# Gate one-hots by pairs of tokens, more U tiles called in the gate steps, dot products of gathered rows behind the V splits

## The chip, the cores and the metric

The kernel is one program on one core of a Trainium2 chip. A core has five engines that run their own instruction streams: TensorE (PE; its weight loads are listed as PEld), VectorE (DVE), ScalarE (ACT), GpSimd (POOL) and SyncE (SP), which issues most DMAs. The metric is the device time of one execution in microseconds (us); less is better. Before the change, three runs gave a median of 2682.41 us (2677.13 to 2683.87).

## The reference

The reference is two transformer blocks on 512 tokens of 1024 features, in fp32. The change touches the last part of the first block, a layer of 16384 experts with one row each in two tables U and V:

```
q = (x @ w_query) -> 8 heads x 2 halves;   s = q . sub_keys        # 128 scores each
top 16 of each half, their 16 x 16 sums, top 16 of those           # 8 heads x 16 experts per token
g = softmax(best);  a = gelu(u[experts] . x);  out = sum(g * a * v[experts])
```

So each token takes 128 of the 16384 experts with weights g. The second block (attention, a recurrence, cross attention and a mixture of 32 experts) isn't touched.

## The kernel before, in words

The expert layer is computed in two ways. For the first three blocks of 128 tokens (384 tokens, `TD`) it is dense: a matrix G of gate weights, 16384 experts by 384 tokens, mostly zero, is built; then U times x, Gelu, times G, and that times V, for all experts. For the fourth block it is sparse: for each of the 128 expert slots of a token, the U row is gathered by an indirect DMA (one row per token, 128 x 1024 numbers) and its dot product with the token is taken on VectorE; later the V row is gathered and added with its weight. That makes 256 gathered rows, in four buffers, the four blocks of the tile `x_sb`.

**Gate steps** (L1172 to L1211). A token's G column is 128 x 128 (the expert's number in two halves), a sum over its 128 slots of products of two one-hot vectors. It is a matmul: the slots lie on the partitions, `oj` is the one-hot of the one half and `o1`, `o2` that of the other times the two parts of the weight. A one-hot of 128 is in turn the product of a one-hot of 8 and one of 16 (the "digits", `digit`, for three chunks of 32 tokens at a time). One step does 8 tokens: three VectorE products (L1197), 16 matmuls of 128 x 128 fp16 (L1205, L1206), two evictions of four tokens each on ScalarE into the staging tile `g_sg` (L1208). 48 steps make 12 chunks; each chunk's 2 MB of `g_sg` go to DRAM (L1211), with two staging tiles. Layout before: four tokens side by side in memory, then the next of the 128 places, so a matmul that takes one token reads fp16 numbers 8 bytes apart. After each third step `u_tile()` is called.

**U tiles** (`u_tile`, L881). One U tile is 128 experts: 512 KB are loaded (three buffers), split into a high part on ScalarE and a low part `w_lo` on VectorE (two buffers each), multiplied in 24 matmuls of 384 columns into PSUM (`b_ups`, two buffers), and Gelu'd on ScalarE into one of 46 places: 10 in `x_sb`, which the gathers need later, and 36 in `b_ab`. A place is free again when the V tile of that number has multiplied it with its gates (`b_wfull`, L945). There are 128 U tiles; 28 calls stand in the program ahead of the gate steps (12 in the selection of the best, 4 and 12 after it), 16 in the gate steps, and a loop fills up to 46.

**V tiles** (`for n in range(128)`, L990 on). Round n loads 512 KB of V (and for each fourth round 768 KB of G), multiplies (`b_wfull`), splits both factors (the low part of V is `b_vl`, on VectorE), and runs 18 matmuls of 512 columns. From round 10 on it also calls `u_tile()`, which does nothing once 128 are done, and then lets gathered rows through: 2.72 a round until round 91, then 1.2, each a gather on POOL's queue (L914) and a dot product (L921) or an addition (L931) on VectorE.

**What sets the order.** The framework schedules at compile time. Each engine's order is worked out from a cost model: of the instructions whose inputs and buffers are there, the one written first in the program goes first, and one that waits for a buffer lets later ones pass. The order is then fixed, and an engine waits in it. Two tools pin an instruction: `keep_in_program_order(i)` puts i behind the instruction of the same engine that was written just before it, and `issue_after(j)` puts all of a block's instructions on j's engine behind j. Both set the order of issue alone. The rows' dot products have the first kind:

```
r = row("u_rows", k)
tc.keep_in_program_order(V.scalar_tensor_tensor(
    junk[:], r, 1.0, h2g[:], op0=OP.mult, op1=OP.mult, accum_out=ag[:, k:k + 1]))
```

Of the kernel before, what the change touches and what calls it, by code (L numbers as in the profile page):

```python
# [13 lines left out]
FP16 = mybir.dt.float16  # L14
# [3 lines left out]
OP = mybir.AluOpType  # L18
# [35 lines left out]
class Kern:  # L54
# [14 lines left out]

    def split(self, src, hi, lo):  # L70
        self.nc.scalar.copy(hi, src)  # L71
        self.nc.vector.tensor_tensor(lo, src, hi, op=OP.subtract)  # L72

    def mm3(self, ps, a, b, start, stop):
        mm = functools.partial(self.nc.tensor.matmul, skip_group_check=True)
# [753 lines left out]
GT = 32  # L829
OG = 8  # L830
DG = 3
# [27 lines left out]
def phase_b(K):  # L859
    nc, tc, d = K.nc, K.tc, K.d  # L860
    V, S, PE = nc.vector, nc.scalar, nc.tensor
    with ExitStack() as st:
        pb = st.enter_context(tc.tile_pool(name="b_pb", bufs=1))
        hT = K.hT
        h2g = K.h2g
        eg = pb.tile([128, 128], I32, name="b_eg")
        gg3 = pb.tile([128, 128], F32, name="b_gg3")
        ag = pb.tile([128, 128], F32, name="b_ag")
# [30 lines left out]
        with ExitStack() as s2:  # L899
# [7 lines left out]
            junk = jp.tile([128, 1024], BF16, name="b_junkg")  # L907
            acc = [[vps.tile([128, 512], F32, name=f"b_acc{b}{h}") for h in range(2)] for b in range(ND)]
            nrow = [0]

            def row(src, k):
                r = K.x[:, nrow[0] % NB]
                nrow[0] += 1
                nc.gpsimd.indirect_dma_start(out=r, out_offset=None, in_=d[src],  # L914
                                             in_offset=bass.IndirectOffsetOnAxis(ap=eg[:, k:k + 1], axis=0))
                return r

            def gather_steps():
                for k in range(128):
                    r = row("u_rows", k)  # L920
                    tc.keep_in_program_order(V.scalar_tensor_tensor(  # L921
                        junk[:], r, 1.0, h2g[:], op0=OP.mult, op1=OP.mult, accum_out=ag[:, k:k + 1]))
                    yield
                S.activation(ag[:], ag[:], AF.Gelu)
                V.tensor_tensor(ag[:], ag[:], gg3[:], op=OP.mult)
                for k in range(128):
                    r = row("v", k)
                    if k == 0:
                        V.tensor_scalar(accg[:], r, ag[:, 0:1], None, op0=OP.mult)
                    else:  # L930
                        tc.keep_in_program_order(V.scalar_tensor_tensor(  # L931
                            accg[:], r, ag[:, k:k + 1], accg[:], op0=OP.mult, op1=OP.add))
                    yield
# [3 lines left out]
            def weighted(n, halves):  # L937

                if n % 4 == 0:
                    g4s[n // 4] = gp.tile([128, TD // GT, 4, GT], F32, name="b_g")  # L940
                    nc.sync.dma_start(g4s[n // 4][:].rearrange("p c i t -> p c (i t)"), gd[n // 4])
                raw = vr.tile([128, 1024], F32, name="b_vraw")
                nc.sync.dma_start(raw[:], d["v"][n * 128:(n + 1) * 128, :])
                f = wf.tile([128, TD], F32, name="b_wfull")
                V.tensor_tensor(f[:].rearrange("p (c t) -> p c t", t=GT), acts[n].rearrange("p (c t) -> p c t", t=GT),  # L945
                                g4s[n // 4][:, :, n % 4], op=OP.mult)
                wh = wsp.tile([128, TD], F32R, name="b_wh")
                wl = wsp.tile([128, TD], F32R, name="b_wl")
                K.split(f[:], wh[:], wl[:])
                vh, vl = halves  # L950
                K.split(raw[:], vh[:], vl[:])
                return wh, wl, vh, vl

            def add_rows(n, t, b, hf):
# [4 lines left out]
            def v_halves():  # L959
                return vs.tile([128, 1024], F32R, name="b_vh"), vs.tile([128, 1024], F32R, name="b_vl")  # L960
# [28 lines left out]
            gs = gather_steps()  # L989
# [4 lines left out]
            for n in range(128):  # L994
                if n < 128 - NLAST:
                    t = weighted(n, v_halves())
# [21 lines left out]
            with in_order(tc):  # L1018
# [4 lines left out]
                f = [finish(b, (accg, h2g)[b % 2], gf, gm, vr.tile([128, 1024], F32, name="b_vraw")) for b in range(ND)]  # L1023
# [4 lines left out]
def peer_gates(K, st, P, hT, small, gd, eg, gg3, u_tile):  # L1028
    nc, tc, d = K.nc, K.tc, K.d
    V, S, PE = nc.vector, nc.scalar, nc.tensor  # L1030
    tk = st.enter_context(tc.tile_pool(name="g_tk", bufs=1))
    tT = tk.tile([128, 6, TD], FP16, name="g_tT")
    rt = tk.tile([128, 16, 16], FP16, name="g_rt")
    with ExitStack() as s0:
# [4 lines left out]
        with ExitStack() as s1:  # L1039
# [18 lines left out]
            for hp in range(16):  # L1058
                w, ps = began.pop(0)
# [25 lines left out]
        for b in range(NB):  # L1085
# [3 lines left out]
            for i in range(5):  # L1089
                n = LENS[i]  # L1090
# [15 lines left out]
        n = NB * 128  # L1106
# [32 lines left out]
        for b in range(NB):  # L1139
# [15 lines left out]
            if b < ND:  # L1155
# [5 lines left out]
                hi = tt[:].bitcast(F32).rearrange("p (a n) -> p a n", a=2)  # L1161
# [5 lines left out]
    with ExitStack() as s2:  # L1167
        ohp = s2.enter_context(tc.tile_pool(name="g_ohp", bufs=2))
        stg = s2.enter_context(tc.tile_pool(name="g_stg", bufs=2))
        gps = s2.enter_context(tc.tile_pool(name="g_gps", bufs=4, space=PSUM))  # L1170
        dg = s2.enter_context(tc.tile_pool(name="g_dg", bufs=1))
        G4 = DG * GT // 4  # L1172
        for c in range(TD // GT):
            if c % DG == 0:
                ts = slice(c * GT, (c + DG) * GT)
                token = lambda w: tT[:, w, ts].rearrange("p (g t) -> p g t", t=4)[:, :, None, :]

                def digit(w, n):

                    t = dg.tile([128, G4, n, 4], FP16, name=f"g_d{w}")  # L1180
                    V.tensor_tensor(t[:], token(w).to_broadcast(t[:].shape),
                                    rt[:, None, 0:n, 0:4].to_broadcast(t[:].shape), op=OP.is_equal)
                    return t[:]

                ih, jh, il, jl = digit(0, 8), digit(1, 8), digit(2, 16), digit(3, 16)
                ih0, ih1 = [dg.tile([128, G4, 8, 4], FP16, name=f"g_d{w}")[:] for w in (4, 5)]
                for w, t in ((4, ih0), (5, ih1)):
                    V.tensor_tensor(t, ih, token(w).to_broadcast(t.shape), op=OP.mult)
            sg = stg.tile([128, 128, GT], F32, name="g_sg")
            for t8 in range(GT // OG):  # L1190
                g0 = ((c % DG) * GT + t8 * OG) // 4
                gs = slice(g0, g0 + OG // 4)
                shape = [128, OG // 4, 8, 16, 4]

                def onehot(hi, lo, name):
                    t = ohp.tile([128, OG // 4, 128, 4], FP16, name=name)
                    V.tensor_tensor(t[:].rearrange("p g (a b) t -> p g a b t", a=8), hi[:, gs, :, None].to_broadcast(shape),  # L1197
                                    lo[:, gs, None].to_broadcast(shape), op=OP.mult)
                    return t

                oj, o1, o2 = onehot(jh, jl, "g_oj"), onehot(ih0, il, "g_o1"), onehot(ih1, il, "g_o2")
                for g in range(OG // 4):
                    ps = gps.tile([128, 4, 128], F32, name="g_gp")
                    for t in range(4):
                        PE.matmul(ps[:, t], oj[:, g, :, t], o1[:, g, :, t], start=True, stop=False)  # L1205
                        PE.matmul(ps[:, t], oj[:, g, :, t], o2[:, g, :, t], start=False, stop=True)  # L1206
                    tq = t8 * OG + 4 * g
                    S.activation(sg[:, :, tq:tq + 4].rearrange("p i t -> p t i"), ps[:], AF.Copy, scale=1.0 / GS)  # L1208
                if (c * (GT // OG) + t8) % 3 == 0:
                    u_tile()  # L1210
            nc.sync.dma_start(gd[:, :, c].rearrange("q p n -> p q n"), sg[:].rearrange("p (q i) t -> p q (i t)", i=4))  # L1211

# [1078 lines left out]
def build(tc, d, out, phases="abcd"):  # L2291
# [3 lines left out]
    with ExitStack() as st:  # L2295
# [16 lines left out]
        with ExitStack() as s1:  # L2312
            if "a" in phases or "b" in phases:
                p2 = s1.enter_context(tc.tile_pool(name="p2", bufs=1))
                K.colsa = p2.tile([128, 27], F32, name="colsa")
                nc.sync.dma_start(K.colsa[:], d["colsa"])
                K.gt2 = p2.tile([128, 1024], F32, name="gt2")
                K.A2 = p2.tile([128, 8], F32, name="A2")
                K.sh2 = p2.tile([128, 8], F32, name="sh2")
                K.h2g = p2.tile([128, 1024], F32, name="h2g")  # L2320
                K.ur = s1.enter_context(tc.tile_pool(name="ur", bufs=3))
                K.us = s1.enter_context(tc.tile_pool(name="us", bufs=2))
                K.xd = s1.enter_context(tc.tile_pool(name="xd", bufs=1, space=DRAM)).tile([NB, 128, 1024], F32, name="xd")
            if "a" in phases:
                phase_a(K)
            elif "b" in phases:
                nc.sync.dma_start(K.gt2[:], bcast_rows(d["gt2_t"], 1024))
                nc.sync.dma_start(K.A2[:], d["A2_t"])
                nc.sync.dma_start(K.sh2[:], d["sh2_t"])
            if "b" in phases:  # L2330
                phase_b(K)
# [28 lines left out]
```

## Time and profile before

| what | value |
|---|---|
| median of three runs | 2682.41 us |
| the profiled execution | 2687.5 us |
| its span, first to last instruction | 2685.7 us |
| mean granted TensorE clock | 0.973 |
| busy: PE, DVE, ACT, POOL | 2548.9, 1782.5, 962.9, 395.8 us |
| gate steps (first to last matmul) | 598.2 to 756.2 us |
| V tiles (first to last matmul) | 774.1 to 1646.3 us |

Times in the rows are us from the span's start unless marked ns. A matmul's record holds its time in the pipe, so neighbours overlap; what one costs in a stream is the distance from start to start. VectorE's records overlap by some 80 ns in the same way. "<-" behind an idle time names what ended it.

### The profile page before, as it was taken

Reading aid. Unit: us, or ns where it says so; the run is one execution under the profiler, and the core shown is the slowest. Engines: PE = TensorE matmul, PEld = TensorE weight load, DVE = VectorE, ACT = ScalarE, POOL = GpSimd, SP = SyncE. Lnnn points to the kernel's source line nnn. Section 1 sums busy time; section 2 is a strip of 40 time slices with the busy share of each in tenths; the row PEclk is TensorE's granted clock in tenths of the full one; section 3 lists DMA queues with packets and bytes.
Section 4 is the critical chain, followed back from the end, with each engine's and each line's share of the span. In section 5 each row is a group of like instructions: output and inputs, shape, how many; then the busy total and the mean of one; then the engine's idle time right before and its main releaser. Section 6 shows DMA issues by size and latency. Waiting matters only on the chain.

```text
span 2685.7 us, 43758 instructions
## 1 busy us (share of the span) xinstructions
PE 2548.9 (95%) x17112; PEld 2122.0 (79%) x17112; DVE 1782.5 (66%) x3794; ACT 962.9 (36%) x1603; POOL 395.8 (15%) x269
## 2 busy tenths in 40 slices
PE   5999999899999999999999998999999989999885
PEld 4976988899978999999999887888797756555664
DVE  6644689987756788778878797567753673333334
ACT  3431442457743333333333335343533421111112
POOL 0000000000013555545555320000000000000001
PEclk8999999999999999999999998898999999999998
DMA  6226222336787989989998883222133489999896
GB/s 232 79 92 210 103 73 80 104 126 188 219 285 273 328 318 329 327 320 323 323 330 317 296 312 122 81 85 74 56 119 114 176 326 387 394 396 360 340 416 260
DMA packets 183485, 623.93 MB, mean 232 GB/s; under 512 B 15847, under 2 KB 66407, under 8 KB 156651
## 3 DMA queue, kind: packets, MB, share of 16 engines
q1 hardware_dynamic: 146410, 486.87, 48.5%
q0 software_dynamic: 36864, 134.23, 14.4%
q8 instruction: 135, 2.21, 0.3%
q14 instruction: 76, 0.61, 0.1%
HBM read 591.55 MB, written 29.49 MB: 231 GB/s over the span
## 4 chain that ended last, share of the span: by engine, by line
PE 83%; DVE 10%; DMA 3%; ACT 2%; issue 2%; SPq 0%; DVEq 0%; ACTq 0%
PE f_hp L1865 6%; PE b_acc L77 6%; PE b_acc L78 6%; PE b_acc L76 6%; PE b_ups L78 6%; PE b_ups L76 6%; PE b_ups L77 6%; PE p_acc L77 5%; PE p_acc L76 5%; PE p_acc L78 5%; PE f_yp L1907 3%; PE f_xp L1764 2%; PE g_gp L1205 2%; PE g_gp L1206 2%; PE f_hp L1851 1%
## 5 line engine op out<-in xcount | busy, mean ns | idle before, releaser
L72 DVE TENSOR_TENSOR w_lo<-w_raw,w_hi 128x1024 fp32r<-128x1024 f32 x228 | 278.0, 1219 | 248.3 <-ACT w_hi L71 248.0
L71 ACT CAST w_hi<-w_raw 128x1024 fp32r<-128x1024 f32 x228 | 239.0, 1048 | 548.4 <-PE b_ups L77 280.9
L78 PE MATMUL b_ups<-hT,w_lo 128*128 128x384 f32 x1024 | 347.8, 340 | 6.6 <-DVE w_lo L72 6.5
L76 PE MATMUL b_ups<-hT,w_hi 128*128 128x384 f32 x1024 | 347.8, 340 | 1.3 <-ACT x_sb L891 1.0
L77 PE MATMUL b_ups<-hT,w_hi 128*128 128x384 f32 x1024 | 345.1, 337 | 0.0
L914 POOL DMA_INDIRECT x_sb<-in_u_rows,b_eg x128 | 197.0, 1539 | 994.5 <-ACT w_hi L71 774.7
L77 PE MATMUL b_acc<-b_vl,b_wh 128*128 128x512 f32 x756 | 297.0, 393 | 9.4 <-DVE b_vl L72 9.3
L76 PE MATMUL b_acc<-b_vh,b_wh 128*128 128x512 f32 x756 | 295.1, 391 | 1.3 <-ACT b_vh L71 1.3
L78 PE MATMUL b_acc<-b_vh,b_wl 128*128 128x512 f32 x756 | 296.1, 392 | 0.0
L77 PE MATMUL p_acc<-w_lo,hT 128*128 128x256 f32 x896 | 255.0, 285 | 7.7 <-DVE w_lo L72 7.7
L76 PE MATMUL p_acc<-w_hi,hT 128*128 128x256 f32 x896 | 255.4, 285 | 2.0 <-ACT hT L71 1.8
L78 PE MATMUL p_acc<-w_hi,hT 128*128 128x256 f32 x896 | 254.3, 284 | 0.0
L914 POOL DMA_INDIRECT x_sb<-in_v,b_eg x128 | 188.6, 1473 | 217.9 <-DVE b_accg L931 189.5
L78 PEld LDWEIGHTS b_ups<-hT,w_lo 128*128 128x128 f32 x1024 | 193.8, 189 | 8.6 <-DVE w_lo L72 8.6
L76 PEld LDWEIGHTS b_ups<-hT,w_hi 128*128 128x128 f32 x1024 | 194.0, 189 | 5.1 <-ACT x_sb L891 1.3
L77 PEld LDWEIGHTS b_ups<-hT,w_hi 128*128 128x128 f32 x1024 | 193.6, 189 | 3.2
L77 PEld LDWEIGHTS p_acc<-w_lo,hT 128*128 128x128 f32 x896 | 171.8, 192 | 13.7 <-DVE w_lo L72 8.2
L71 ACT CAST b_wh<-b_wfull 128x384 fp32r<-128x384 f32 x128 | 65.6, 514 | 320.1 <-PE b_acc L77 314.9
L76 PEld LDWEIGHTS p_acc<-w_hi,hT 128*128 128x128 f32 x896 | 171.5, 192 | 7.6 <-issue 3.9
L78 PEld LDWEIGHTS p_acc<-w_hi,hT 128*128 128x128 f32 x896 | 171.7, 192 | 4.2 <-issue 3.4
L921 DVE SCALAR_TENSOR_TENSOR b_junkg<-x_sb,h2g 128x1024 bf16<-128x1024 f32 x128 | 156.3, 1221 | 25.7 <-DMA x_sb<-in_u_rows,b_eg 24.1
L77 PEld LDWEIGHTS b_acc<-b_vl,b_wh 128*128 128x128 f32 x756 | 142.9, 189 | 38.1 <-DVE b_vl L72 11.1
(659 smaller groups left out, 5101.6 us busy)
## 6 DMA issues: line engine op xcount, KB each, us to landing
f_w<-in_w SPq DMA_DIRECT2D x192, 1024.0 KB, 10.4
w_raw<-in_u SPq DMA_DIRECT2D x128, 512.0 KB, 5.6
b_vraw<-in_v SPq DMA_DIRECT2D x128, 512.0 KB, 6.5
b_gd<-g_sg SPq DMA_DIRECT2D x12, 2048.0 KB, 9.1
b_g<-b_gd SPq DMA_DIRECT2D x32, 768.0 KB, 8.0
a_ar_t<-in_w_ada SPq DMA_DIRECT2D x32, 512.0 KB, 4.3
w_raw<-in_w_tok SPq DMA_DIRECT2D x20, 512.0 KB, 3.6
a_ar_t<-in_w_ada SPq DMA_DIRECT2D x8, 1024.0 KB, 8.2
```

Source lines behind the costliest of these rows:

```text
L71: self.nc.scalar.copy(hi, src)
L72: self.nc.vector.tensor_tensor(lo, src, hi, op=OP.subtract)
L76: first = mm(ps, a[0], b[0], start=start, stop=False)
L77: mm(ps, a[0], b[1], start=False, stop=False)
L78: mm(ps, a[1], b[0], start=False, stop=stop)
L914: nc.gpsimd.indirect_dma_start(out=r, out_offset=None, in_=d[src], in_offset=bass.IndirectOffsetOnAxis(ap=eg[:, k:k + 1], axis=0))
L921: tc.keep_in_program_order(V.scalar_tensor_tensor(junk[:], r, 1.0, h2g[:], op0=OP.mult, op1=OP.mult, accum_out=ag[:, k:k + 1]))
L1205: PE.matmul(ps[:, t], oj[:, g, :, t], o1[:, g, :, t], start=True, stop=False)
L1206: PE.matmul(ps[:, t], oj[:, g, :, t], o2[:, g, :, t], start=False, stop=True)
L1764: PE.matmul(room[k // 4][:, k % 4, :n], hs[i][:, b, k * 128:(k + 1) * 128], sel[:, b, :n], start=k % 4 == 0 and i == 0 and b == 0, stop=i ...
L1865: last = PE.matmul(p, X[:, k], ts["w31", k // 2][:, c0:c0 + 512], start=k == 0, stop=k == 7, skip_group_check=True)
L1907: PE.matmul(p, gT[k], ts["w2", hf][:, k * 512:(k + 1) * 512], start=k == 0, stop=k == 3, skip_group_check=True)
```

## The change

Three edits. The gate one-hots and their digits are laid out with two tokens side by side instead of four, so that a matmul reads numbers 4 bytes apart; the number of elements per VectorE instruction and the matmuls stay. `u_tile()` is called after four of five gate steps (38 calls) instead of one of three (16). And `split` returns its VectorE instruction, the V split's is kept in `split[0]`, and the rows' U dot products are also put behind it with `issue_after`.

```
     def split(self, src, hi, lo):
         self.nc.scalar.copy(hi, src)
-        self.nc.vector.tensor_tensor(lo, src, hi, op=OP.subtract)
+        return self.nc.vector.tensor_tensor(lo, src, hi, op=OP.subtract)
...
+            split = [None]
...
                     r = row("u_rows", k)
-                    tc.keep_in_program_order(V.scalar_tensor_tensor(
-                        junk[:], r, 1.0, h2g[:], op0=OP.mult, op1=OP.mult, accum_out=ag[:, k:k + 1]))
+                    with tc.issue_after(split[0].ins):
+                        tc.keep_in_program_order(V.scalar_tensor_tensor(
+                            junk[:], r, 1.0, h2g[:], op0=OP.mult, op1=OP.mult, accum_out=ag[:, k:k + 1]))
...
-                K.split(raw[:], vh[:], vl[:])
+                split[0] = K.split(raw[:], vh[:], vl[:])
...
-                token = lambda w: tT[:, w, ts].rearrange("p (g t) -> p g t", t=4)[:, :, None, :]
+                token = lambda w: tT[:, w, ts].rearrange("p (g t) -> p g t", t=2)[:, :, None, :]
...
-                    t = dg.tile([128, G4, n, 4], FP16, name=f"g_d{w}")
+                    t = dg.tile([128, GN, n, 2], FP16, name=f"g_d{w}")
...
-                shape = [128, OG // 4, 8, 16, 4]
+                shape = [128, OG // 2, 8, 16, 2]
...
-                    t = ohp.tile([128, OG // 4, 128, 4], FP16, name=name)
+                    t = ohp.tile([128, OG // 2, 128, 2], FP16, name=name)
...
-                    for t in range(4):
-                        PE.matmul(ps[:, t], oj[:, g, :, t], o1[:, g, :, t], start=True, stop=False)
-                        PE.matmul(ps[:, t], oj[:, g, :, t], o2[:, g, :, t], start=False, stop=True)
+                    for q in range(4):
+                        j, t = divmod(4 * g + q, 2)
+                        PE.matmul(ps[:, q], oj[:, j, :, t], o1[:, j, :, t], start=True, stop=False)
+                        PE.matmul(ps[:, q], oj[:, j, :, t], o2[:, j, :, t], start=False, stop=True)
...
-                if (c * (GT // OG) + t8) % 3 == 0:
+                if (c * (GT // OG) + t8) % 5:
                     u_tile()
```

## Rows read from the trace of the kernel before

**Rows 1.** By stretch: length, busy (count) of PE, PEld, DVE, ACT, POOL, clock, DMA share, GB/s.
```profile
598.20:756.40 158.20, 158.20 (x1156) 149.78 (x1156) 115.31 (x172) 118.09 (x130) 0.00 (x0) 1.00 0.67 203
...
774.10:843.20 69.10, 59.70 (x241) 47.92 (x242) 44.31 (x66) 22.36 (x32) 18.05 (x14) 0.93 0.79 295
...
790.70:796.30 5.60, 5.59 (x13) 4.48 (x14) 2.58 (x4) 0.00 (x0) 1.88 (x2) 0.50 0.81 300
...
847.30:1498.70 651.40, 651.40 (x3317) 595.17 (x3316) 520.65 (x649) 228.26 (x317) 335.14 (x215) 1.00 0.90 323
```

**Rows 2.** The chain of waits between the stages: start, us, what.
```profile
757.55 9.29 DMA b_gd<-g_sg
767.00 4.55 DMA b_g<-b_gd
...
780.73 7.46 DMA x_sb<-in_u_rows,b_eg
```

**Rows 3.** VectorE in order of time, at three places of the V stage.
```profile
803.95 0.56 DVE L945 TENSOR_TENSOR b_wfull<-b_a,b_g 128x384 f32<-128x384 f32 x1
...
847.43 1.23 DVE L72 TENSOR_TENSOR w_lo<-w_raw,w_hi 128x1024 fp32r<-128x1024 f32 x1 [2.46 <-ACT w_hi L71]
848.57 1.22 DVE L921 SCALAR_TENSOR_TENSOR b_junkg<-x_sb,h2g 128x1024 bf16<-128x1024 f32 x1
...
1508.09 1.22 DVE L72 TENSOR_TENSOR b_vl<-b_vraw,b_vh 128x1024 fp32r<-128x1024 f32 x1
1509.23 1.28 DVE L931 SCALAR_TENSOR_TENSOR b_accg<-x_sb,b_ag,b_accg 128x1024 f32<-128x1024 f32 x1
```

**Rows 4.** ScalarE in order of time: start, us, engine, line, what, idle time before.
```profile
761.18 0.49 ACT L891 ACTIVATE b_a<-b_ups 128x384 f32<-128x384 f32 x1
...
765.34 0.49 ACT L891 ACTIVATE b_a<-b_ups 128x384 f32<-128x384 f32 x1
...
804.54 0.49 ACT L891 ACTIVATE b_a<-b_ups 128x384 f32<-128x384 f32 x1 [1.65 <-DVE b_wfull L945]
```

**Rows 5.** TensorE in order of time: two gate matmuls, and L1764.
```profile
752.25 0.28 PE L1205 MATMUL g_gp<-g_o,g_oj 128*128 128x128 f16 x1
...
755.91 0.29 PE L1206 MATMUL g_gp<-g_o,g_oj 128*128 128x128 f16 x1
...
2195.64 3.75 PE L1764 MATMUL f_xp<-f_sel,f_hs 128*128 128x128 f16 x64
```

**Rows 6.** Weight loads of the gate matmuls and of L1764: ns min/median/max.
```profile
L1205 PEld LDWEIGHTS <-g_oj x384: 113/117/138, 598.2 to 755.7; 128*128 128x128 f16 x192
...
L1764 PEld LDWEIGHTS <-f_hs x896: 95/98/181, 2162.5 to 2609.7; 128*128 128x128 f16 x180
```

**Rows 7.** Groups by shape in the gate stage, VectorE and ScalarE; then four evictions together.
```profile
L1197 DVE TENSOR_TENSOR g_o<-g_d,g_d 128x1024 f16<-128x1024 f16 x96 | 61.8, 683 | 0.0
...
L1181 DVE TENSOR_TENSOR g_d<-g_tT,g_rt 128x1536 f16<-128x1536 f16 x8 | 7.4, 957 | 0.0
L1181 DVE TENSOR_TENSOR g_d<-g_tT,g_rt 128x768 f16<-128x768 f16 x8 | 4.4, 563 | 0.0
L1188 DVE TENSOR_TENSOR g_d<-g_d,g_tT 128x768 f16<-128x768 f16 x8 | 4.1, 549 | 0.0
...
753.61 3.92 ACT L1208 ACTIVATE g_sg<-g_gp 128x512 f32<-128x512 f32 x4
```

**Rows 8.** Windows of L921 (two records per row), then of L931 (one).
```profile
774.10:843.20 69.10, 12.30 (x20) 0.93 0.79 295
843.20:1437.00 593.80, 145.02 (x236) 1.00 0.90 322
...
843.20:1437.00 593.80, 97.23 (x76) 1.00 0.90 322
```

**Rows 9.** DMA issues by line: engine, count, us from issue to landing.
```profile
x_sb<-in_v,b_eg POOLq DMA_INDIRECT x128, 7.3
```

**Rows 10.** The page, part 5: line, what, count, busy us, mean ns, idle before.
```profile
L914 POOL DMA_INDIRECT x_sb<-in_v,b_eg x128 | 188.6, 1473 | 217.9 <-DVE b_accg L931 189.5
```

More of the change, by code (lines that the diff above doesn't have):

```diff
@@ L1171, in peer_gates @@
         dg = s2.enter_context(tc.tile_pool(name="g_dg", bufs=1))
-        G4 = DG * GT // 4
+        GN = DG * GT // 2
         for c in range(TD // GT):
@@ L1175, in peer_gates @@
                 ts = slice(c * GT, (c + DG) * GT)
-                token = lambda w: tT[:, w, ts].rearrange("p (g t) -> p g t", t=4)[:, :, None, :]
+                token = lambda w: tT[:, w, ts].rearrange("p (g t) -> p g t", t=2)[:, :, None, :]
                 def digit(w, n):
-                    t = dg.tile([128, G4, n, 4], FP16, name=f"g_d{w}")
+                    t = dg.tile([128, GN, n, 2], FP16, name=f"g_d{w}")
                     V.tensor_tensor(t[:], token(w).to_broadcast(t[:].shape),
-                                    rt[:, None, 0:n, 0:4].to_broadcast(t[:].shape), op=OP.is_equal)
+                                    rt[:, None, 0:n, 0:2].to_broadcast(t[:].shape), op=OP.is_equal)
                     return t[:]
                 ih, jh, il, jl = digit(0, 8), digit(1, 8), digit(2, 16), digit(3, 16)
-                ih0, ih1 = [dg.tile([128, G4, 8, 4], FP16, name=f"g_d{w}")[:] for w in (4, 5)]
+                ih0, ih1 = [dg.tile([128, GN, 8, 2], FP16, name=f"g_d{w}")[:] for w in (4, 5)]
                 for w, t in ((4, ih0), (5, ih1)):
@@ L1190, in peer_gates @@
             for t8 in range(GT // OG):
-                g0 = ((c % DG) * GT + t8 * OG) // 4
-                gs = slice(g0, g0 + OG // 4)
-                shape = [128, OG // 4, 8, 16, 4]
+                g0 = ((c % DG) * GT + t8 * OG) // 2
+                gs = slice(g0, g0 + OG // 2)
+                shape = [128, OG // 2, 8, 16, 2]
                 def onehot(hi, lo, name):
-                    t = ohp.tile([128, OG // 4, 128, 4], FP16, name=name)
+                    t = ohp.tile([128, OG // 2, 128, 2], FP16, name=name)
                     V.tensor_tensor(t[:].rearrange("p g (a b) t -> p g a b t", a=8), hi[:, gs, :, None].to_broadcast(shape),
```

## The prediction

> **What bounds the kernel now.** I read the page's first part first: TensorE is busy for most of the span, so nearly everything that is saved has to be TensorE time or TensorE idle time. Then the table by stage [rows 1], which holds the two stages that the change touches. In the gate stage (598.2 to 756.4) TensorE is busy 158.2 of 158.2 us at full clock, VectorE 115.3 and ScalarE 118.1: TensorE bounds it. At the head of the V stage (774.1 to 843.2) TensorE is busy only 59.7 of 69.1 us and the mean granted clock is 0.93; after that, in 847.3 to 1498.7, busy all the time, with the DMA engines at 0.90 and 323 GB/s.
>
> In the chain of waits the gate stage ends in a DMA to DRAM and one back (9.29 and 4.55 us), and the head of the V stage in a gathered row that lands 7.46 us after its issue [rows 2]. The order on VectorE [rows 3] shows what ties a row's dot product: it comes right behind `w_lo` of the U tile that is called in the same round (847.43, 848.57), and, when no U tile is left, right behind `b_vl` of the round (1508.09, 1509.23). That is `keep_in_program_order`: an edge to the VectorE instruction written just before. It decides this forecast.
>
> Unit prices. A U tile is 4.16 us of TensorE (two neighbours, 761.18 and 765.34) [rows 4]. A pair of U and V tile is 8.25 us (651.4 us for 79 pairs) [rows 1], so a V tile is 4.09. A gate matmul is 0.118 us: 31 steps from 752.25 to 755.91 [rows 5].
>
> **Part 1, pairs of tokens.** 768 gate matmuls now step 8 bytes from column to column, then 4. The nearest fp16 matmuls of the same size, L1764, read neighbouring columns: 64 in 3.75 us, 0.058 each [rows 5]. The weight load hardly differs between the two (117 and 98 ns) [rows 6], so I put the doubling down to the moving operand. [...] A gate step of 16 falls from 1.89 to 0.93 us.
> [...]
> VectorE writes the same number of elements per one-hot, 683 ns [rows 7]. No row has an inner run of two. [...]
>
> **Part 2, U tiles in the gate steps.** 28 U tiles stand in the program ahead of the gate steps. `% 5` calls 38 in 48 steps, `% 3` called 16. But only 46 outputs have a place (10 in `x_sb`, 36 in `b_ab`), and two more wait in PSUM: already now the Gelu of the 47th waits for the product of V tile 10 (804.54 behind 803.95) [rows 3, 4]. So 48 U tiles are multiplied ahead of the V stage before and after. In the program numbers 28 to 47 now fall into the first 25 steps: 20 x 4.16 + 25 x 0.93 = 106.4 us, from 598.2 to 704.6. The 23 steps left have no U tile. VectorE: 23 x 3 x 0.60 (683 ns less the 80 by which its records overlap) + 4.0 for one group of digits ((7.4 + 4.4 + 4.1)/4) = 45.4 us; ScalarE: 46 evictions of 0.98 (3.92 for four) = 45.1 [rows 7]; the writes of `g_sg`, two buffers, some 8 us to fill and 9.29 to land, (8 + 9.3)/2 = 8.65 per four steps, 49.7. I take 49.7: the last eviction ends at 754.3 instead of 757.55. Bounds 45 (750) and, with a matmul of 0.118, 131 + 50 from 598.2 (779). Halving the gate matmuls thus gives 3.3 us, as the steps without U tiles are not TensorE's. The DMA pair of 16.6 us until the first V matmul (774.14) is covered now by four U tiles and then by nothing; it costs no more, but TensorE starts cold: 2.6 us, as between 790.7 and 796.3, where the clock was 0.50 and 13 matmuls took 0.43 instead of 0.23 [rows 1].
>
> **Part 3, dot products behind the V split.** Before, 10 rows came into the first 13 V tiles [rows 8], because the U tile of their round (46 to 49) had long been split. Those rows made the stalls: 69.1 us for 13 x 4.09 = 53.2, so 15.9 lost, and all of it goes. But not by the new edge. In round 10 the program now calls U tile 66, not 46, so the first dot product stands behind `w_lo` of U tile 66. That needs tile 64 multiplied, thus 62's Gelu, thus the product of V tile 26, which runs when TensorE is in V tile 21 (tile 10's ran at 803.95 in V tile 5: 93 matmuls of 18 each had started). U tiles run 8 rounds earlier than now (48 after V tile 4, now after 12), and the rows some 11 rounds later. The edge to `b_vl` is weaker and binds nowhere.
>
> So 16 pairs pass with no gather on the DMA queues. Rows of round n stand behind U tile 56 + n up to round 71; when the last `w_lo` (U 127) is done, TensorE is in V tile 82, and 62 x 2.72 = 168 rows have been let through. TensorE gets there at 754.3 + 16.6 + 2.6 + 83 x 4.09 + 79 x 4.16 = 1441.6. Before, at 1437, 10 + 118 + 76 = 204 rows were done [rows 8].
>
> The rest is 45 V tiles, one U tile and 88 rows. TensorE alone: 45 x 4.09 + 4.16 = 188, done at 1630, 16 before the 1646 of now. VectorE: 88 x 1.2 + 45 x (1.14 + 2 x 0.47) = 199 [rows 3]. DMA: 88 x 0.524 MB + 42 x 0.721 MB (three V tiles are loaded by then; 0.524 of V, a fourth of 0.786 of gates) = 76.4 MB at 323/0.90 = 359 GB/s = 213 [rows 1]. The four row buffers: (7.3 landing + 1.3 dot product + 1.5 issue)/4 = 2.5 us per row, 222 [rows 3, 9, 10]. The pace that was held before, 593.8/194 = 3.06 us, gives 269 [rows 8]. The row instructions come earlier in the program than the V splits that are left, so the backlog is served first and TensorE waits for V splits. I take 2.45 us x 88 = 216 (between DMA and buffers), and 12 us for some three V tiles that come out behind the last row (bounds 0 and 8 tiles, 33 us): 1669.6, 23 us later than now. Row sums and the three normalisations follow as now.
>
> **Sum.** -3.3 (gates) + 2.6 (cold start) - 15.9 (stalls) + 40 (rows late: 1669.6 against 1630) = +23. The profiled execution took 2687.5 us with a span of 2685.7, 5.1 above the median 2682.4. 2687.5 + 23 - 5.1 = 2705.
>
> **Rivals.**
> A, forecast: rows late, 2705. Its own range goes from DMA-bound without a gap (1441.6 + 213 = 1654.6, +8) to the pace of before and three tiles (1722.6, +76, of which I keep +50): 2690 to 2732.
> B: the debt is served dense, splits slip between the rows, and faster DMA than 359 GB/s (the head of the stage moved 295 at 0.79, 373 for a full share) ends the stage between 1638 and 1654: -8 to +8, some 2680. For it: the DMA work is the same in sum. Against: 88 rows in 45 tiles are two per tile, and both VectorE (199) and DMA (205 to 213) are over TensorE's 188.
> C, the other side: the dot products are not late, or their lateness costs nothing, since the order keeps V splits ahead. Then TensorE bounds to the end: 1630, -16.6, 2666. It decides if the rows' rate in the last 45 tiles can reach 188/88 = 2.1 us. Against: no stretch of before shows it.
> D: the 4-byte step doesn't speed the matmul up: 25 steps of 1.89 add 24, on top of A: 2729.
> [...]
>
> **Chances.** A 0.52, B 0.17, C 0.13, D 0.12, E 0.06. Of C, 0.01 ends within 0.3%. A measurement of this kernel tells about 0.3% (8 us) from no change. Slower: A, D, E = 0.70; same: B and that 0.01 = 0.18; faster 0.12. Range: 2672 leaves out most of C, 2740 E and a little of D.
>
> **What would show it.** Gate matmuls 0.058 apart in the trace (else D); one-hots 683 ns (else E). U Gelus every 5.3 us until about 704, none in the rest of the gate stage, and a TensorE gap of some 18 us ahead of the first V matmul. No row before TensorE is in V tile 20; a first Gelu of the V stage as V tile 5 runs, the last near 1445. From there dot products in the idle column of VectorE, and TensorE idle on `b_vl`. I am wrong if rows start near V tile 10, or if TensorE stays busy from 1441 on.

## The result, and the profile after

The changed kernel took 2816.18 us (median of four, 2812.9 to 2829.0) beside 2683.14 for the kernel before: 1.0485 times as long [1.0458, 1.0513], slower by 133 us. The forecast was slower, 2705, with a range to 2740. The sign held, and so did one of its causes, the late rows. The size was short by 111 us, the time lies outside the range, and most of what is missing came from a place that the forecast had priced at nothing: the pairs of U and V tiles while the rows run.

The profiled execution has a span of 2817.6 us, 131.9 more than before. The last V matmul ends at 1778.2 instead of 1646.3, which is the same 131.9: nothing behind the expert layer moved. (The gate steps begin at 602.3 in this execution, at 598.2 in the one before, so some 4 us had come ahead of them.) First the stages, in the columns of [rows 1]: the gate steps, their second part, the V stage without rows, with rows, and after the last U tile.

```profile
602.30:757.60 155.30, 140.03 (x1249) 131.06 (x1248) 125.02 (x176) 119.49 (x134) 0.00 (x0) 0.96 0.72 219
705.00:757.60 52.60, 37.33 (x408) 31.42 (x406) 48.19 (x76) 44.40 (x48) 0.00 (x0) 0.87 0.88 260
775.20:843.20 68.00, 67.60 (x307) 57.25 (x308) 31.98 (x42) 24.24 (x33) 4.99 (x4) 0.95 0.56 197
843.20:945.00 101.80, 101.23 (x501) 88.73 (x500) 40.57 (x47) 34.99 (x48) 0.00 (x0) 1.00 0.42 147
945.00:1547.80 602.80, 554.32 (x2691) 494.96 (x2690) 423.89 (x562) 188.32 (x259) 251.67 (x176) 0.97 0.79 283
1550.00:1778.20 228.20, 189.20 (x728) 146.81 (x727) 197.32 (x248) 70.08 (x103) 96.06 (x76) 0.90 0.85 307
```

The V stage starts where it did (774.1 before), and its head has no stalls any more: 67.6 of 68.0 us busy, before 59.7 of 69.1 [rows 1]. The fifth line is the news. A pair of U and V tile is 42 matmuls, so 2691 of them are 64.1 pairs in 602.8 us, 9.41 each; before they took 8.25. TensorE is idle for 48.5 us there, and its mean clock is 0.97. DMA is less busy than before (0.79, before 0.90). The U Gelus on ScalarE, in the columns of [rows 4], show where the stretch ends:

```profile
700.68 0.49 ACT L891 ACTIVATE b_a<-b_ups 128x384 f32<-128x384 f32 x1
...
800.66 0.49 ACT L891 ACTIVATE b_a<-b_ups 128x384 f32<-128x384 f32 x1 [0.26 <-DVE b_wfull L947]
809.23 0.49 ACT L891 ACTIVATE b_a<-b_ups 128x384 f32<-128x384 f32 x1 [0.26 <-DVE b_wfull L947]
...
1547.76 0.49 ACT L891 ACTIVATE b_a<-b_ups 128x384 f32<-128x384 f32 x1
```

The last is at 1547.76; the forecast had it near 1445, and that gap of 103 us is nearly all of the miss (111). Pairs take 8.57 us from 800 on, already without rows. VectorE in order of time, two pairs inside the slow stretch (columns of [rows 3]):

```profile
1131.33 1.23 DVE L72 TENSOR_TENSOR w_lo<-w_raw,w_hi 128x1024 fp32r<-128x1024 f32 x1 [4.43 <-ACT w_hi L71]
1132.47 1.22 DVE L923 SCALAR_TENSOR_TENSOR b_junkg<-x_sb,h2g 128x1024 bf16<-128x1024 f32 x1
...
1136.15 1.22 DVE L72 TENSOR_TENSOR w_lo<-w_raw,w_hi 128x1024 fp32r<-128x1024 f32 x1
...
1138.43 1.22 DVE L72 TENSOR_TENSOR b_vl<-b_vraw,b_vh 128x1024 fp32r<-128x1024 f32 x1
1140.26 1.22 DVE L923 SCALAR_TENSOR_TENSOR b_junkg<-x_sb,h2g 128x1024 bf16<-128x1024 f32 x1 [0.62 <-DMA x_sb<-in_u_rows,b_eg]
...
1142.00 0.56 DVE L947 TENSOR_TENSOR b_wfull<-b_a,b_g 128x384 f32<-128x384 f32 x1
...
1142.95 1.22 DVE L72 TENSOR_TENSOR b_vl<-b_vraw,b_vh 128x1024 fp32r<-128x1024 f32 x1
1144.08 0.55 DVE L947 TENSOR_TENSOR b_wfull<-b_a,b_g 128x384 f32<-128x384 f32 x1
1148.56 1.23 DVE L72 TENSOR_TENSOR w_lo<-w_raw,w_hi 128x1024 fp32r<-128x1024 f32 x1 [3.93 <-ACT w_hi L71]
```

Two U splits stand together with the rows tied to them, then two V splits, and the two gate products (`b_wfull`) come last. Before, one U split and one V split alternate. VectorE's compiled order says the same (w is `w_lo`, V `b_vl`, f `b_wfull`, l `b_wl`, r one or more rows):

```
before  VfwrlrVfwrlrVfwrlfVwrlrVfwrlrVfwrlfVwrlr
after   VflfVwrwrlrVrlfVfwrwrVrlrVlflfVwrwrwrlrV
```

The waits of 945 to 1340, in which dot products run in the kernel after all the time (who waits, for whom, us in total, times, longest):

```profile
ACT w_hi L71 <- PE b_ups L77: 114.7, 36, 6.6
DVE w_lo L72 <- ACT w_hi L71: 84.0, 25, 7.1
...
ACT b_a L891 <- DVE b_wfull L947: 52.5, 23, 6.2
DVE b_junkg L923 <- DMA x_sb<-in_u_rows,b_eg: 34.2, 23, 3.3
PEld b_ups L76 <- ACT b_a L891: 21.6, 14, 4.2
PEld b_acc L77 <- DVE b_vl L72: 18.8, 10, 4.2
```

Read from below it is a ring: TensorE waits for the Gelu that frees its PSUM buffer, the Gelu for the gate product that frees its place, that product stands on VectorE behind the rows, a row waits for its gather, and the next U split waits for TensorE (`w_hi` on ScalarE, and `w_lo` behind it). VectorE's 34.2 us of waits for gathers are about TensorE's 33.0 idle us of that window (below); that the two numbers match doesn't show yet that the one causes the other.

### The profile page after: what moved, and what is told of

The parts are those of the page before. It is cut to its first block, busy times and chain, and to the rows that moved or that the text cites. A ratio compares the mean times of both kernels' runs of the same rounds, so it can differ in the third digit from the quotient of the medians.

```text
span 2817.6 us, 43621 instructions
## 1 busy us (share of the span) xinstructions
PE 2569.2 (91%) x17112; PEld 2108.1 (75%) x17112; DVE 1789.4 (64%) x3794; ACT 965.7 (34%) x1603; POOL 363.6 (13%) x269
## 4 chain that ended last, share of the span: by engine, by line
PE 53%; issue 18%; DMA 13%; DVE 11%; POOL 3%; ACT 2%; SPq 0%; DVEq 0%; POOLq 0%; ACTq 0%
PE f_hp L1868 6%; DMA x_sb<-in_v,b_eg 6%; DMA x_sb<-in_u_rows,b_eg 5%; PE p_acc L77 5%; PE p_acc L76 5%; PE p_acc L78 5%; PE f_yp L1910 3%; POOL x_sb L915 3%; PE b_ups L76 2%; PE b_ups L78 2%; PE b_ups L77 2%; PE f_xp L1767 2%; PE f_hp L1854 1%; DVE w_lo L72 1%; PE p_one L607 1%
## 5 line engine op out<-in xcount | busy, mean ns | idle before, releaser
L76 PE MATMUL b_ups<-hT,w_hi 128*128 128x384 f32 x1024 | 358.0, 350 | 27.0 <-ACT b_a L891 24.5
L77 PE MATMUL b_acc<-b_vl,b_wh 128*128 128x512 f32 x756 | 310.4, 411 | 57.4 <-DVE b_vl L72 56.9
L77 PE MATMUL b_ups<-hT,w_hi 128*128 128x384 f32 x1024 | 351.3, 343 | 0.0
L915 POOL DMA_INDIRECT x_sb<-in_u_rows,b_eg x128 | 185.0, 1445 | 1195.7 <-ACT b_wh L71 775.8
L78 PE MATMUL b_acc<-b_vh,b_wl 128*128 128x512 f32 x756 | 306.3, 405 | 0.0
L76 PE MATMUL b_acc<-b_vh,b_wh 128*128 128x512 f32 x756 | 281.6, 397 | 22.7 <-ACT b_vh L71 17.4
L76 PEld LDWEIGHTS b_ups<-hT,w_hi 128*128 128x128 f32 x1024 | 198.3, 194 | 44.4 <-ACT b_a L891 41.4
L77 PEld LDWEIGHTS b_ups<-hT,w_hi 128*128 128x128 f32 x1024 | 198.3, 194 | 0.4
L915 POOL DMA_INDIRECT x_sb<-in_v,b_eg x128 | 168.4, 1315 | 180.4 <-DVE b_accg L933 155.7
L933 DVE SCALAR_TENSOR_TENSOR b_accg<-x_sb,b_ag,b_accg 128x1024 f32<-128x1024 f32 x127 | 162.8, 1282 | 42.1 <-DMA x_sb<-in_v,b_eg 41.0
L76 PEld LDWEIGHTS b_acc<-b_vh,b_wh 128*128 128x128 f32 x756 | 144.7, 192 | 55.4 <-ACT b_vh L71 17.6
L76 PEld LDWEIGHTS p_acc<-w_hi,hT 128*128 128x128 f32 x896 | 171.2, 191 | 8.1 <-issue 4.2
```

The costliest lines, as they stand in the source:

```text
L76: first = mm(ps, a[0], b[0], start=start, stop=False)
L77: mm(ps, a[0], b[1], start=False, stop=False)
L78: mm(ps, a[1], b[0], start=False, stop=stop)
L933: tc.keep_in_program_order(V.scalar_tensor_tensor(accg[:], r, ag[:, k:k + 1], accg[:], op0=OP.mult, op1=OP.add))
```

## The experiments

The ratios are to the kernel before on the same chip, with 95% intervals. For "us per pair", the matmuls in 945 to 1340 are divided by 42.

| kernel | median us | ratio | us per pair, 945 to 1340 |
|---|---|---|---|
| after | 2816.2 | 1.0485 [1.0458, 1.0513] | 9.44 |
| layout alone | 2670.8 | 0.9942 [0.9918, 0.9967] | |
| edge alone | 2676.5 | 0.9943 [0.9913, 0.9973] | |
| calls alone | 2849.6 | 1.0614 [1.0570, 1.0659] | |
| after, calls held at 46 | 2673.7 | 0.9936 [0.9912, 0.9959] | 8.25 |
| held at 48 | 2677.6 | 0.9957 [0.9931, 0.9984] | 8.25 |
| held at 56 | 2789.2 | 1.0366 [1.0302, 1.0430] | 9.39 |
| rows ahead of the U call | 2710.0 | 1.0064 [1.0035, 1.0093] | 8.56 |
| held at 46, rows from round 21 | 2715.6 | 1.0101 [1.0064, 1.0139] | 8.25 |
| rows not pinned | 2838.4 | 1.0575 [1.0538, 1.0613] | |
| no gathers of U rows | 2763.9 | 1.0298 [1.0267, 1.0330] | 8.36 |
| held at 46, rows every second round | 2675.3 | 0.9953 [0.9927, 0.9980] | 8.25 |
| 40 places, four row buffers | 2825.2 | 1.0511 [1.0470, 1.0552] | 9.36 |
| 40 places, six row buffers | 2725.9 | 1.0143 [1.0099, 1.0187] | 8.36 |
| held at 46 and spread | 2655.3 | 0.9878 [0.9845, 0.9910] | 8.24 |

**Which part of the change?** The kernel after with one edit: the gate steps call no U tile past the 46 places.

```
-            peer_gates(K, s1, P, hT, small, gd, eg, gg3, u_tile)
+            peer_gates(K, s1, P, hT, small, gd, eg, gg3, lambda: len(acts) < NAB + NX and u_tile())
```

> The kernel after, but no call in the gate steps goes past the 46th U tile, so that round 10 of the V stage calls U tile 46 again and not 66. Theory T1 (the 20 calls past the places put every later U tile 20 calls earlier in the program, and with it the rows some 11 rounds late and the U and V splits in clumps): the V stage is back at the pace of before, 8.25 us a pair, and only the head without rows (about -10 to -16) and the gates (-3, cold start +3) are left: 2662 to 2685 us. Rival T2 (the 4-byte layout or the edge behind the V split disturbs the V stage): stays near 2816. Rival T3 (U tiles bunched in the first half of the gate steps): near 2816 too.

And each hunk of the change by itself on the kernel before: the layout,

```
-    t = ohp.tile([128, OG // 4, 128, 4], FP16, name=name)
+    t = ohp.tile([128, OG // 2, 128, 2], FP16, name=name)
```

> The kernel before with the pair layout of the one-hots alone (one U tile after each third gate step, no edge behind the V split). T1: the gate matmuls save 768 x 0.06 = 46 us of TensorE in a stage that TensorE bounds, until ScalarE (118 us busy) and VectorE (115) bound it: the stage goes from 158 to 120 to 130 us, and nothing else changes: 2645 to 2660. T2: slower than before. T3: the same as T1.

the calls,

```
-                if (c * (GT // OG) + t8) % 3 == 0:
+                if (c * (GT // OG) + t8) % 5:
```

> The kernel before with U tiles called after four of five gate steps alone (8-byte layout, no edge). T1: the rise of the kernel after, plus some 22 us for the gate steps at the old matmul price (25 x 1.89 + 20 x 4.16 = 130, then 50): 2815 to 2845. T2: the layout or the edge is missing, so about 2683 to 2710. T3: as T1.

and the edge.

```
+                    with tc.issue_after(split[0].ins):
```

> The kernel before with the edge of the dot products behind the V split alone. T1: it takes the first rows out of the head of the V stage, at most the 16 us of stalls there, 2667 to 2683, or it binds nowhere and the time is 2683. T2 (the edge disturbs the stage): 2750 or more.

The capped kernel took 2673.7, with 8.25 us a pair:

```profile
945.00:1340.00 395.00, 395.00 (x2012) 360.71 (x2011) 315.67 (x408) 139.57 (x193) 204.50 (x131) 1.00 0.92 325
```

The calls alone cost as much as the whole change and 1.3% (35 us) more, where 22 us were expected for the 8-byte step; that is 5 us above the expected range. Layout and edge each gain some 15 us. So the 20 calls past the places are the whole loss, T1, and T2 and T3 fall. The layout gained less than expected (2645 to 2660 was forecast). The profile of the layout alone, in the columns of [rows 1], shows what then bounds its gate steps:

```profile
598.20:729.40 131.20, 121.68 (x1154) 111.44 (x1154) 120.23 (x172) 113.59 (x127) 0.00 (x0) 0.96 0.79 237
```

They take 131.2 us instead of 158.2, where 120 to 130 were expected, with TensorE no longer always busy and VectorE at 120.2. That execution was 31 us shorter than the one profiled before, the median of ten only 15; the rest of that difference is not explained here.

**Late, tied, or ahead?** Three theories of what 20 early calls do. First, all calls stay, but each round lets its rows through ahead of its U call, so that they stand behind `b_vl`:

```
-                if n >= NX:
-                    u_tile()
                 due += 0 if n < NX else PACE if n < 128 - NAB else 1.2
                 while done < min(int(due), 256):
                     next(gs)
                     done += 1
+                if n >= NX:
+                    u_tile()
```

> The kernel after, all 38 calls kept, but each round of the V stage lets its rows through ahead of its U call, so that a dot product is tied to b_vl of its own round and no longer to w_lo of U tile 56 + n. Theory T-rank (the rows, tied to a U tile that was called some 10 rounds before it can run, stand in VectorE's order as a backlog ahead of the V splits around them, and the splits wait there behind gathers): the U tiles called ahead do no harm by themselves, pairs return to 8.25 to 8.6 us and the time to 2665 to 2695. Rival T-late (what costs is that the first row starts at V tile 20 and fewer rounds are left): the rows start at V tile 8 to 10 again, the same 2665 to 2695. Rival T-U (U tiles called 20 rounds ahead outrank the V splits on VectorE and ScalarE): stays at 2780 to 2816.

Then the capped kernel with rows as late as after, each in its own round's place:

```
-                due += 0 if n < NX else PACE if n < 128 - NAB else 1.2
+                due += 0 if n < 21 else PACE if n < 114 else 1.2
```

> The kernel after with the calls held at 46 U tiles until the V stage, and the rows let through from round 21 on instead of round 10, 2.72 a round until round 113 and 1.2 after that; the last row keeps its round (116 to 119). So the rows start as late as in the kernel after, but each stands in its own round's place in the program. T-rank: late rows in their right place cost little, pairs stay at 8.25 us and the end moves by the 11 rounds' rows at most: 2670 to 2700. T-late: lateness is the price: 2760 to 2816. T-U: no U tile is ahead: 2670 to 2690.

And half the dose of calls (`len(acts) < 56` in the lambda above).

> The kernel after with the calls in the gate steps held at 56 U tiles, 10 past the 46 places instead of 20, so that round n calls U tile 46 + n. All three theories give a part of the rise: by the number of calls past the places half of the way from the capped kernel to the kernel after, 2730 to 2760; if the rise has a threshold (the places' 10 rounds of slack), near 2680.

Moving the rows takes away 4.2 of the 4.85%; what stays at 2710.0, above the expectation, is mostly 8.56 us a pair: the matmuls of a U tile wait for the Gelu that frees their PSUM buffer, 46 times in 945 to 1340, and no dot product waits for a gather there.

```profile
PEld b_ups L76 <- ACT b_a L891: 21.7, 46, 0.5
```

Late rows alone cost 1.0101 against 0.9936, 1.65% or 44 us, between T-rank's and T-late's numbers: pairs keep 8.25 us, and the loss is behind the last U tile, as its two stretches show.

```profile
945.00:1485.00 540.00, 540.00 (x2752) 493.53 (x2751) 431.47 (x552) 188.95 (x262) 281.75 (x180) 1.00 0.91 325
1485.00:1676.00 191.00, 160.35 (x656) 125.77 (x654) 162.78 (x211) 63.72 (x97) 71.87 (x57) 0.96 0.81 289
```

656 matmuls are 36.4 V tiles, 149 us of work at 4.09, in 191 us. Half the calls give not half but over three quarters of the loss from the capped kernel to the one after (0.0430 of 0.0549): a miss for all three theories. Its pairs are already as slow as those of the kernel after (9.39 beside 9.44), so between 48 and 56 calls the whole price of a pair is reached; what it saves lies behind the last U tile, where 179.3 us pass for 39.7 V tiles (162 us of work).

**The tie, the order, or the gathers?** The dot products without either pin:

```
-                    with tc.issue_after(split[0].ins):
-                        tc.keep_in_program_order(V.scalar_tensor_tensor(
-                            junk[:], r, 1.0, h2g[:], op0=OP.mult, op1=OP.mult, accum_out=ag[:, k:k + 1]))
+                    V.scalar_tensor_tensor(
+                        junk[:], r, 1.0, h2g[:], op0=OP.mult, op1=OP.mult, accum_out=ag[:, k:k + 1])
```

> The kernel after with the dot products not pinned at all (neither behind the instruction written before them nor behind the V split); the U calls past the places stay. In the compiled order of VectorE two U splits stand in a row with rows between them and the V splits of two rounds follow together, as in the kernel after, but from V tile 3 on, and the order is strictly alternating only once the dot products are done. Theory T-order (with U tiles called past the places the planner puts two U tiles and then two V tiles together whenever rows stand between the splits, and TensorE waits on the splits): still slow, 2740 to 2800, with the pairs slow from some 790 to 1100 us instead of 945 to 1548. Theory T-pin (the tie to w_lo is what costs): back to 2660 to 2700.

All U-row gathers but four left out:

```
+                if src == "u_rows" and k >= NB:
+                    return r
                 nc.gpsimd.indirect_dma_start(out=r, out_offset=None, in_=d[src],
```

> The kernel after, but of the 128 gathers of U rows only the first four are issued; all 128 dot products stay, on whatever the four buffers hold, and VectorE's compiled order is that of the kernel after. It leaves out 124 gathers of 0.52 MB. T-order: the two U splits in a row and the Gelu that waits for a gate product behind them remain, so the pairs of 945 to 1400 us stay above 8.8 us; the rows' lateness goes in part, as 65 MB of DMA fall away: 2730 to 2790. T-gather (VectorE's waits for gathered rows, with V splits queued behind them, make the pairs slow): pairs at 8.25 to 8.6 us while the dot products run, and 2700 to 2730.

Two calls past the places, which PSUM holds (`len(acts) < 48`).

> The kernel after with the calls in the gate steps held at 48 U tiles, the 46 places and the two that can wait in PSUM. T-order: the compiled order of VectorE still alternates (one U split, one V split), so this is the capped kernel, 2665 to 2685, and the harm begins between 48 and 56. Rival T-dose (each call past the places costs alike, some 10 us as between 46 and 56): 2690 to 2700.

Without pins it got worse (2838.4, above T-order's range too), so the tie to `w_lo` isn't the cause. Its windows while dot products run, and after them without rows:

```profile
775.00:1110.00 335.00, 287.87 (x1316) 251.74 (x1316) 258.04 (x388) 93.50 (x126) 173.18 (x131) 0.94 0.90 323
1114.00:1400.00 286.00, 284.33 (x1405) 249.30 (x1404) 118.15 (x136) 101.25 (x134) 1.66 (x2) 1.00 0.47 154
```

1316 matmuls are 31.3 pairs at 10.7 us, 1405 are 33.5 at 8.55. The two calls that PSUM holds do no harm. The kernel without gathers split my theory: the time fell inside T-order's range, but the pairs went as T-gather said. VectorE's compiled order is that of the kernel after, and yet (this kernel first, then the kernel after):

```profile
945.00:1340.00 395.00, 393.90 (x1985) 354.11 (x1984) 307.62 (x445) 139.12 (x190) 4.38 (x3) 1.00 0.47 155
```

```profile
945.00:1340.00 395.00, 361.96 (x1758) 322.81 (x1756) 275.36 (x396) 123.58 (x168) 164.97 (x114) 0.97 0.79 283
```

47.3 pairs against 41.9. So the clumped order costs 0.1 us a pair by itself, and 1.2 with gathers in it.

That kernel is still 77 us slower than before because its rows are late all the same. From the last U Gelu to the last V matmul it takes as long as the kernel after, for as many V tiles, where the capped kernel runs at TensorE's own pace (without gathers, after, capped):

```profile
1495.30:1722.90 227.60, 189.01 (x741) 146.89 (x739) 198.16 (x248) 71.11 (x105) 96.91 (x77) 0.93 0.87 310
1547.80:1778.40 230.60, 191.60 (x739) 148.55 (x737) 198.34 (x248) 70.84 (x106) 96.73 (x77) 0.90 0.85 307
...
1498.40:1646.20 147.80, 147.76 (x656) 122.08 (x654) 129.84 (x181) 61.04 (x94) 32.55 (x28) 1.00 0.77 271
```

741 and 739 matmuls are 41 V tiles, 168 us of work at 4.09, so some 60 us are lost there in both; in the capped kernel 656 matmuls (36.4 tiles, 149 us) lose nothing. The loss of the kernel after thus has two parts, slow pairs ahead of the last U tile and late rows behind it.

**Clumps, buffers or the queues?** The other half of the cross: U calls in their places, rows in clumps.

```
-                while done < min(int(due), 256):
+                while (n % 2 or n > 117) and done < min(int(due), 256):
```

> The capped kernel (no U tile past the 46 places), but rows are let through only in every second round, five or six at once instead of two or three each round; the U and V splits keep their places. T-clump (a clump of over four rows waits for gathers, since there are four row buffers, and the splits behind it wait with it): the pairs with rows go from 8.25 to 8.6 to 9.5 us, 2700 to 2780. T-splits (clumped rows do no harm as long as U and V splits alternate): 2665 to 2685.

And the kernel after with room for two more row buffers, without and with them:

```
-NAB = 36
+NAB = 30
...
+            more = [jp.tile([128, 1024], F32, name=f"b_more{i}")[:] for i in range(2)]
...
-                r = K.x[:, nrow[0] % NB]
+                i = nrow[0] % (NB + 2)
+                r = K.x[:, i] if i < NB else more[i - NB]
```

> Control for the next run: the kernel after with 30 instead of 36 places in b_ab (which makes room for two row buffers), the calls in the gate steps held at 60 (20 past the 40 places, as 66 are past 46), and the rows' pace kept to round 92. Six U tiles fewer are multiplied ahead of the V stage and six more in it. VectorE's compiled order has the same pattern, so all theories: 2800 to 2830.

> The control with six row buffers instead of four. T-clump: more gathers are under way ahead of a clump, VectorE's waits for gathered rows (37.7 us in 945 to 1450 of the kernel after) shrink by half or more, and pairs with dot products return towards 8.6 us: 40 to 80 below the control. T-dma (the load of the queues, not the buffers, makes them late): within 10 us of the control. T-splits (two U splits and a Gelu behind a gate product that stands behind the rows): within 20 of the control.

Two buffers gave back 99 of the 136 us that the control lies above before, more than expected (40 to 80). Of the 99, 22 lie behind the last U Gelu (164.6 us to the last V matmul instead of 186.9), as six buffers help the late rows too; the stretch from the first V matmul to that Gelu gave 73. The control and the six, in the same window:

```profile
945.00:1340.00 395.00, 362.03 (x1772) 323.53 (x1771) 279.07 (x401) 124.79 (x169) 168.93 (x117) 0.98 0.80 284
```

```profile
945.00:1340.00 395.00, 393.91 (x1984) 353.99 (x1983) 307.45 (x442) 138.67 (x190) 197.48 (x129) 1.00 0.88 321
```

The queues moved 321 GB/s instead of 284 once they were given earlier gathers, so their load was not the limit (T-dma falls), and no dot product waits for a gather any more (32.7 us in the control). But rows in bursts with alternating splits did no harm at all, against T-clump, although VectorE waited for gathers there too:

```profile
DVE b_junkg L923 <- DMA x_sb<-in_u_rows,b_eg: 27.5, 22, 3.3
```

```profile
945.00:1340.00 395.00, 395.00 (x2012) 360.91 (x2011) 315.37 (x410) 139.67 (x193) 186.48 (x131) 1.00 0.91 324
```

27.5 us of waits, and TensorE busy for all 395. So neither half is enough: in an alternating order late gathers were absorbed (8.25), the clumped order is nearly free with punctual gathers (8.36), and together they cost 9.4.

One rival stays open. In the run with bursts the U tiles also keep to their places, so no Gelu waits for a gate product (52.5 us in the kernel after). Whether the alternating order or this slack absorbed the late gathers, no run separates: alternating splits with U tiles past the places were seen only where no gather was late, at 8.55 to 8.57 us a pair (the kernel after ahead of 945, rows not pinned after 1114, rows ahead of the U call).

**A better version.** The change, with 18 calls spread over the 48 steps and none past the places:

```
-                if (c * (GT // OG) + t8) % 5:
+                if (c * (GT // OG) + t8) % 8 in (0, 3, 5):
```

> The kernel after with 18 U calls spread evenly over the 48 gate steps (steps 0, 3 and 5 of each eight) and none past the 46 places. Theory: gates as with the pair layout alone (last gate matmul near 729, first V matmul near 748 instead of 774), the stalls at the head of the V stage gone by the edge (-10), V stage at 8.25 us a pair: 2640 to 2660, 25 to 45 below before. Rival: the gains don't add, since the head of the V stage waits for the G write and the V load either way: 2660 to 2675.

2655.3 us, 0.9878 of before, as expected: the gains of layout and edge add. Its last gate matmul starts at 738.0 and the first V matmul at 758.2 (expected near 729 and 748; the gate steps begin 4.6 us later in this execution), the last U Gelu at 1470.6 (1498.5 before).

## Why the prediction was wrong, step by step

- **Part 1 held.** In the kernel after, eleven gate matmuls follow the first of these two, the last 0.65 us later:

```profile
640.26 0.23 PE L1208 MATMUL g_gp<-g_o,g_oj 128*128 128x128 f16 x1
...
640.91 0.22 PE L1209 MATMUL g_gp<-g_o,g_oj 128*128 128x128 f16 x1
```

  0.059 each; the 0.93 us a step stand on the 0.058 of L1764 [rows 5]. Rival D falls: with the 8-byte step a gate matmul took 0.118 us [rows 5], twice as long. One-hots with runs of two stayed at 683 ns [rows 7], so rival E, which has them take longer on VectorE, falls. The comparisons that make the digits did take longer: 957 ns before for 128x1536 [rows 7], 1721 ns in the kernel after.

```profile
L1199 DVE TENSOR_TENSOR g_o<-g_d,g_d x96: 678/683/755, 587.9 to 754.4; 128x1024 f16<-128x1024 f16 x96
```

- **Part 2 held.** The gate matmul behind the last U tile of the gate steps stands at 710.0, 107.7 us after the first one (forecast 106.4), the last eviction ends 49.6 us after that, at 759.6 (forecast 49.7), and the first V matmul stands at 775.2 (forecast 754.3 + 16.6 + 2.6 = 773.5).

```profile
710.02 0.23 PE L1208 MATMUL g_gp<-g_o,g_oj 128*128 128x128 f16 x1
...
754.13 5.47 ACT L1211 ACTIVATE g_sg<-g_gp 128x512 f32<-128x512 f32 x6
```

  In 705.0 to 757.6, which holds the last U tile too, VectorE is busy 48.2 of 52.6 us and DMA at 0.88, near the forecast's bounds (VectorE 45, the writes of `g_sg` 50 us).
- **Part 3, head and first row, held.** The stalls are gone and the first dot product comes at 945.3 with TensorE in V tile 22 (399 V matmuls), where V tile 21 was forecast (773.5 + 21 x 4.09 + 16 x 4.16 = 926 at its prices). That the new edge binds nowhere in the kernel after was not tried by itself; on the kernel before it moves the first row from 781.7 to 819.4 and gains 15 us, which the prediction put down to the calls.
- **The step that failed: "TensorE gets there at 754.3 + 16.6 + 2.6 + 83 x 4.09 + 79 x 4.16 = 1441.6".** It carried the unit prices of [rows 1], 8.25 a pair, over to an order that it had itself described as changed, put no wait on TensorE while the rows run, and asked of the late rows only how many are left at the end. With the last U tile (4.16) the sum gives 1445.8; the last U Gelu came at 1547.8, 102 us later. Of these, 74 are the 64.1 pairs at 9.41 instead of 8.25 (48.5 of TensorE idle, the rest busy time), 5 the 16 pairs without rows at 8.57, 7 the first U tile of the V stage at 800.7 (773.5 and five V tiles, 794, in the sum), and 16 some 3.9 V tiles more than forecast that were done by then: 739 matmuls from 1547.8 on are 41.1 tiles, not 45. Those 16 us shortened nothing, as the rows set the length of the stretch behind.
- **The term "rows late" was right in length and short in cost.** The stretch behind the last U tile took 228.2 us (1441.6 to 1669.6, 228, was forecast), with 80 rows left instead of 88, and additions 2.40 us apart (76 from 1559.1 to 1739.4) instead of 2.45. But TensorE had 168 us of work left there and not 188, so the term, forecast as +40, came to some 62. Late rows in their places cost 44 in all.
- **Rivals B and C** fell, as row debt did cost time. No rival had pairs slower while rows run, so the range ended 76 us short of the time. The direction didn't hang on the pairs: with punctual gathers they were nearly free, and the kernel was still slower (2763.9), by its late rows.

## What to carry to other kernels

Calling work earlier in the program than its buffers allow does not run it before a buffer is free (48 U tiles were multiplied ahead of the V stage before and after): it gives that work a rank ahead of what frees its buffers, and with rows between the splits the planner packed the fixed order in clumps here. Hold such calls at the places there are (46 or 48 did no harm here, 56 cost 4%). A unit price read from a stage need not hold for another order of its engines (8.25 us a pair before, 9.41 after): when a change shifts that order, ask how much slack each in-order wait then has. And where waits for gathers show up in a slow stretch, look whether anything can absorb them before adding buffers: 27.5 us of such waits were free where the splits alternated and U tiles had places to spare, and 34.2 us went with 33 us of idle TensorE in 395 where neither was so.

## What the runs showed of the hardware that was not expected

The weight load of the gate matmuls fell with the step as well, from 117 to 97 ns [rows 6], where the prediction put the whole doubling down to the moving operand. Which of the two reads set the 0.118 us no run separates; after the change the loads, at 97 ns, are longer than the 59 ns between matmuls, so their records overlap.

```profile
L1208 PEld LDWEIGHTS <-g_oj x384: 96/97/149, 602.3 to 757.4; 128*128 128x128 f16 x192
```

And behind some idle stretches of TensorE the granted clock was 0.50 here, so they were paid for twice. One such place in the slow pairs, in the columns of [rows 1]:

```profile
1293.00:1299.70 6.70, 3.10 (x10) 2.20 (x9) 5.82 (x10) 2.29 (x4) 4.42 (x3) 0.79 0.86 298
1299.70:1303.60 3.90, 3.90 (x13) 3.58 (x12) 0.76 (x1) 0.15 (x1) 0.00 (x0) 0.50 0.94 349
1303.60:1307.00 3.40, 3.40 (x21) 3.40 (x20) 0.00 (x0) 0.52 (x1) 0.00 (x0) 0.98 0.07 24
```

TensorE was idle for 3.6 of 6.7 us, then did 13 matmuls in 3.9 us at a granted clock of 0.50, and 21 in the next 3.4 at 0.98. Over the whole stretch 64.1 pairs took 554.3 busy us, 8.65 each and not 8.25: of the 74 us, 26 were busy time and not idle time. The clock's mean of 0.97 makes some 16 of them (an estimate, 3% of 554.3). The rest isn't the clock: in 843.2 to 945.0, at a clock of 1.00, a pair already took 8.49 busy us, and with rows ahead of the U call TensorE shows 392.75 of 395 us busy in 945 to 1340 beside 21.7 us of waits of at most 0.5 us, which the busy share hides.
